# One 128 x 128 scaling per chunk of the RWKV operand [b|k]: GpSimd's TENSOR_SCALAR becomes ScalarE's ACTIVATE

## The chip, the cores and the metric

The kernel runs on one core of a Trainium2 chip. The metric is device time in microseconds (us) of one execution; lower is better. The kernel before took 1404.71 us (median of three runs, 1403.94 to 1408.78).

## The reference: what is computed

One hybrid transformer block over 512 tokens of width 1024, float32. The input is normed and multiplied by `w_in`; three mixers use slices of the result (HGRN2, RWKV-7 and a latent attention, MLA); their outputs are multiplied by branch weights, gated and summed; an output projection and a gated feed-forward layer follow, each with a norm and a residual.

```python
h = rms_norm(x, mix_pre_g[l])
z = h @ w_cols
o_hg = hgrn2_mixer(zq, zf, zi, zog, ...)
o_rw, v_first = rwkv7_mixer(zrw, rwkv_mu[l], ...)
o_mla = mla_mixer(zcq, zckv, zkr, cos, sin, ...)
merged = (g_hg * (o_hg @ w_branch[l, 0]) + g_rw * (o_rw @ w_branch[l, 1])
          + g_mla * (o_mla @ w_branch[l, 2]))
x = x + rms_norm(merged @ w_out[l], mix_post_g[l])
x = x + rms_norm((silu(gate) * up) @ w_ffn_out[l], ffn_post_g[l])
```

The change lies in the RWKV mixer, whose state is updated token by token in the reference:

```python
sa = jnp.einsum('bhvk,bhk->bhv', state, -kk_t)
state = (state * w_t[:, :, None, :] + sa[..., None] * (kk_t * a_t)[:, :, None, :]
         + v_t[..., None] * k_t[:, :, None, :])
```

The kernel does this by chunks of 64 tokens. For each chunk it needs the matrix [b|k] (b is `kk * a`), scaled so that the decay runs to the end of the next chunk. That scaling, one factor for each of 128 channels and each chunk, is what the change moves.

## The kernel before

**Dense products.** All large products run as three TensorE passes: each float32 operand is split into a high part (rounded to fp32r) and a low part, and `mm3` (lines 137, 138 and 139) issues high x high, low x high and high x low into one PSUM tile. A weight slab of 128 x 2 x 256 is loaded by a DMA from SyncE's queue (`wsD`), rounded on ScalarE (`whD`, line 205), and its low part is made on VectorE (`wlD`, line 132). Slabs have three buffers. `stream` walks an output of 256 columns: for each slab two column blocks, for each block two groups of three matmuls. The two PSUM tiles (`mmD`, a pool of two buffers) are copied out on ScalarE when complete (`zst`, line 237, or a tanh at line 251 for the gates) and written to DRAM.

**Tokens.** The dense stream is the filler behind everything else. So that it cannot run ahead, `pace` (line 141) makes each group write a token, a 1 x 1 memset on GpSimd (line 149) that waits for the group's last matmul. The first matmul of a group waits for the token of the group five before it (`PACE = 5`). GpSimd executes in order, so a token stands behind whatever GpSimd is doing.

**RWKV preparation.** Eight pairs of heads (p from 0 to 7) in four groups are prepared while the input projection streams. In `rwkv_prep`, `BK` is a tile of 8 chunks of 128 x 128. It is first the stationary operand of the score products with X (lines 578 to 582, recorded at lines 191 and 194, the lines of a helper that keeps pairs side by side). VectorE masks the scores out of PSUM (lines 584, 585). Then seven of the chunks are scaled in place by the next chunk's decay, `gC[:, c + 1]`, at line 594. They are transposed on TensorE, four at a time and then three, and copied to the group's tile `G` by ScalarE (line 599). `BK` and most temporaries have one buffer. The result goes to DRAM (`rwd`) and is read back in the serial chain over chunks, `rwkv_chain`, which starts after the fourth group.

**Other uses of GpSimd.** It also computes the power -1/2 for every norm (line 279), small memsets (lines 521, 640), and in the chain the decay of the state (line 717).

**Order of the work.** The program is written in lanes: each lane is a range of priorities, and a scheduler with its own estimate of durations sets the order of the instructions on each engine when the kernel is built. Every engine then executes its list in order, waiting where operands are not ready. MLA, in the second half, is interleaved with the dense products of branches 0, 1 and 2 in the same way.

Of the kernel before, what the change touches and what calls it, by code (L numbers as in the profile page):

```python
# [16 lines left out]
AF = mybir.ActivationFunctionType  # L17
ALU = mybir.AluOpType
# [84 lines left out]
class Kern:  # L103
# [391 lines left out]
    def rwkv_prep(self, G, p, q):  # L495
        nc, rt = self.nc, self.rt
        V, A, Pl = nc.vector, nc.scalar, nc.gpsimd
# [34 lines left out]
        gC = self.gC[:, p]  # L532
# [28 lines left out]
        BK = self.t(rt, [P, NC, P], "BK")  # L561
# [29 lines left out]

        n = NC - 1
        for c in range(n):
            Pl.tensor_scalar(BK[:, c], BK[:, c], gC[:, c + 1:c + 2], None, op0=ALU.mult)  # L594
        for cc in range(0, n, 4):
            m = min(4, n - cc)
            pt = self.t(self.pR, [P, 4, P], "pr")
# [768 lines left out]
```

## Time and profile before

| | |
|---|---|
| median of three runs | 1404.71 us |
| lowest, highest | 1403.94, 1408.78 us |
| the profiled execution, its time | 1408.42 us |
| span of its profile | 1406.6 us |
| mean granted TensorE clock | 0.996 |
| TensorE matmul busy | 1354.8 us, 96% of the span |
| VectorE busy | 848.3 us, 60% |
| ScalarE busy | 638.6 us, 45% |
| GpSimd busy | 190.8 us, 14% |
| the changed operation (line 594) | 56 instructions, 47.0 us busy on GpSimd |

Engines are named PE (TensorE matmul), PEld (its weight loads), DVE (VectorE), ACT (ScalarE), POOL (GpSimd) and SP (SyncE). Rows of groups read: line, engine, operation, output <- inputs, shapes, count, then busy us and mean ns of one, then the idle time of the engine just before and what ended it. Matmuls are pipelined and their ends are modelled, so PE at 96% is not PE at its peak; what the profile tells well is when PE had nothing under way. Rows of the waits read: who waited, for whom, total us, times, longest.

### The profile page before, as it was taken

What the parts mean: (1) busy time and instruction counts of PE and PEld (TensorE: products, weight loads), DVE (VectorE), ACT (ScalarE), POOL (GpSimd) and SP (SyncE); (2) the same over time, 40 slices, a digit from 0 to 9 for tenths busy, and PEclk for the clock granted to TensorE, in tenths of its full rate; (3) what the DMA queues carried; (4) which work ended last, traced back from release to release, by engine and by line L of the source; (5) the groups of instructions that cost most, each with busy time, mean ns of one, the idle gap of its engine ahead of it and who ended that gap; (6) DMA issues with size and microseconds to landing.
All of it is one profiled execution on the core that took longest, in us unless ns stands there. A gap on an engine that the chain in (4) does not pass through costs nothing.

```text
span 1406.6 us, 27356 instructions
## 1 busy us (share of the span) xinstructions
PE 1354.8 (96%) x9664; PEld 1103.2 (78%) x9664; DVE 848.3 (60%) x1756; ACT 638.6 (45%) x1259; POOL 190.8 (14%) x1042
## 2 busy tenths in 40 slices
PE   6999999999999999999999999999999999999998
PEld 5777777777777777888788888877888888888886
DVE  5567797797787784575665576655575344343234
ACT  5554546556556453433665354443354333332222
POOL 2122132131222311242210000001010000000000
PEclk9999999999999999999999999999999999999999
DMA  5565467557755777986464555415544333334233
GB/s 180 149 193 144 129 183 227 178 153 218 213 157 155 242 237 227 356 277 208 137 204 147 157 178 168 130 53 173 198 139 135 98 97 92 102 95 156 97 98 105
DMA packets 196025, 231.62 MB, mean 165 GB/s; under 512 B 42672, under 2 KB 137392, under 8 KB 195888
## 3 DMA queue, kind: packets, MB, share of 16 engines
q1 hardware_dynamic: 194496, 226.72, 52.1%
q10 hardware_dynamic: 1392, 3.15, 0.7%
q8 instruction: 76, 1.25, 0.4%
q14 instruction: 61, 0.50, 0.1%
HBM read 169.65 MB, written 60.16 MB: 163 GB/s over the span
## 4 chain that ended last, share of the span: by engine, by line
PE 82%; DMA 6%; DVE 4%; issue 4%; ACT 3%; POOL 1%; SPq 1%; POOLq 0%; DVEq 0%; ACTq 0%
PE mmD L137 18%; PE mmD L138 17%; PE mmD L139 17%; PE po L137 4%; PE po L139 4%; PE po L138 4%; PE pr L194 1%; DMA wsD<-in_w_in_dram 1%; DMA z<-zst 1%; DMA zr<-z 1%; PE pmo L1138 1%; PE pm L137 1%; PE pm L139 1%; PE pm L138 1%; PE ph L843 1%
## 5 line engine op out<-in xcount | busy, mean ns | idle before, releaser
L137 PE MATMUL mmD<-xH,whD 128*128 128x512 f32 (+1 forms) x1232 | 486.2, 397 | 11.9 <-POOL token L149 5.6
L138 PE MATMUL mmD<-xL,whD 128*128 128x512 f32 (+1 forms) x1232 | 474.2, 386 | 0.0
L139 PE MATMUL mmD<-xH,wlD 128*128 128x512 f32 (+1 forms) x1232 | 469.6, 385 | 0.9 <-DVE wlD L132 0.9
L132 DVE TENSOR_TENSOR wlD<-wsD,whD 128x512 fp32r<-128x512 f32 x384 | 263.2, 687 | 292.0 <-ACT whD L205 276.0
L205 ACT CAST whD<-wsD 128x512 fp32r<-128x512 f32 x384 | 236.7, 618 | 375.8 <-PE mmD L138 244.1
L137 PEld LDWEIGHTS mmD<-xH,whD 128*128 128x128 f32 x1232 | 232.0, 189 | 65.2 <-POOL token L149 8.9
L139 PEld LDWEIGHTS mmD<-xH,wlD 128*128 128x128 f32 x1232 | 232.2, 189 | 48.6 <-DVE wlD L132 2.0
L138 PEld LDWEIGHTS mmD<-xL,whD 128*128 128x128 f32 x1232 | 233.5, 190 | 40.1
L149 POOL MEMSET token<- 1x1 f32 x912 | 82.2, 90 | 675.4 <-PE mmD L139 660.1
L139 PE MATMUL po<-whD,fL 128*128 128x512 f32 x176 | 68.6, 390 | 0.0
L138 PE MATMUL po<-wlD,fH 128*128 128x512 f32 x176 | 68.6, 390 | 0.0
L137 PE MATMUL po<-whD,fH 128*128 128x512 f32 x176 | 61.9, 390 | 0.0
L279 POOL TENSOR_TENSOR rrs<-rtm,mhalf 128x1 f32<-128x1 f32 x8 | 4.4, 551 | 402.3 <-DVE rtm L274 368.7
L646 DVE TENSOR_TENSOR invtmp<-inv 64x30 f32<-64x30 f32 (+14 forms) x120 | 38.7, 322 | 17.7 <-DMA inv<-Ld 16.0
L594 POOL TENSOR_SCALAR BK<-BK,gC 128x128 f32<-128x128 f32 x56 | 47.0, 854 | 11.8 <-PE pr L194 11.8
L237 ACT COPY zst<-mmD 128x512 f32<-128x512 f32 x64 | 37.3, 583 | 14.6 <-PE mmD L139 14.4
L647 DVE TENSOR_TENSOR inv<-inv,invtmp 64x30 f32<-64x30 f32 (+14 forms) x120 | 38.4, 320 | 2.2
L139 PEld LDWEIGHTS po<-whD,fL 128*128 128x128 f32 x176 | 33.0, 188 | 7.0
L138 PEld LDWEIGHTS po<-wlD,fH 128*128 128x128 f32 x176 | 33.0, 188 | 7.0
L137 PEld LDWEIGHTS po<-whD,fH 128*128 128x128 f32 x176 | 33.0, 188 | 7.0
L843 PEld LDWEIGHTS ph<-hq,hk 128*32 128x32 f32 x1536 | 17.6, 111 | 18.0 <-issue 9.6
L1136 ACT COPY mpT<-pmt 128x128 f32<-128x128 f32 (+3 forms) x32 | 13.6, 425 | 38.0 <-PE pmt L1134 37.9
(349 smaller groups left out, 1960.1 us busy)
## 6 DMA issues: line engine op xcount, KB each, us to landing
wsD<-in_w_in_dram SPq DMA_DIRECT2D x176, 256.0 KB, 3.4
wsD<-in_w_ffn_in_dram SPq DMA_DIRECT2D x96, 256.0 KB, 2.8
z<-zst SPq DMA_DIRECT2D x63, 256.0 KB, 3.3
rwd<-G SPq DMA_DIRECT2D x28, 512.0 KB, 5.5
G<-rwd SPq DMA_DIRECT2D x28, 512.0 KB, 6.7
wsD<-in_w_branch_dram SPq DMA_DIRECT2D x48, 256.0 KB, 2.9
wsD<-in_w_ffn_out_dram SPq DMA_DIRECT2D x44, 256.0 KB, 2.6
zr<-z SPq DMA_DIRECT2D x26, 256.0 KB, 3.3
```

What stands on the lines that cost most here:

```text
L132: (eng or self.nc.vector).tensor_tensor(dst, src, high.bitcast(F32), op=ALU.subtract)
L137: first = mm(ps, lhsT=lh, rhs=rh, start=start, stop=False)
L138: mm(ps, lhsT=lh, rhs=rl, start=False, stop=False)
L139: return first, mm(ps, lhsT=ll, rhs=rh, start=False, stop=stop)
L149: token = self.nc.gpsimd.memset(self.token, 0.0).ins
L194: last = c()
L205: nc.scalar.copy(h, st)
L237: self.nc.scalar.copy(st[:m], ps)
L594: Pl.tensor_scalar(BK[:, c], BK[:, c], gC[:, c + 1:c + 2], None, op0=ALU.mult)
L646: V.tensor_tensor(tv, cv, rv, op=ALU.mult)
L647: V.tensor_tensor(U[:, :j, j + 1:], U[:, :j, j + 1:], tv, op=ALU.add)
L843: mm(g[b:b + HB, o // P, :], lhsT=k[:, t], rhs=q[:, t], start=True, stop=True)
```

## The change

In the loop over seven chunks of each of the eight pairs, the multiplication by the per-partition scalar is issued on ScalarE as a Copy with a scale instead of on GpSimd:

```diff
         n = NC - 1
         for c in range(n):
-            Pl.tensor_scalar(BK[:, c], BK[:, c], gC[:, c + 1:c + 2], None, op0=ALU.mult)
+            A.activation(BK[:, c], BK[:, c], AF.Copy, scale=gC[:, c + 1:c + 2])
         for cc in range(0, n, 4):
             m = min(4, n - cc)
             pt = self.t(self.pR, [P, 4, P], "pr")
             self.side_by_side(partial(nc.tensor.transpose, pt[:, c], BK[:, cc + c, :], self.ident) for c in range(m))
             A.copy(G["BKT"][:, q, cc:cc + m, :], pt[:, :m])
```

Since the scheduler works from all instructions together, other rows move too. In the program the first pairs keep nearly their order but for the moved operation; from the fourth pair on, matmuls, casts and copies are interleaved differently.

On GpSimd, in the preparation of pair 1 (BK is the operand, token the pacing memset, rs and lw small tiles of the preparation, inv the tile of the inverse), the piece of the difference is:

```order
 L279 TENSOR_TENSOR rs_4895<-ss_4893,mhalf 128x8
-L149 MEMSET token 1x1 x21
-L594 TENSOR_SCALAR BK_4905<-BK_4905,gC_4658 128x128 x4
-L149 MEMSET token 1x1 x4
-L594 TENSOR_SCALAR BK_4905<-BK_4905,gC_4658 128x128 x3
-L149 MEMSET token 1x1 x6
+L149 MEMSET token 1x1 x31
 L640 MEMSET inv_5012 64x32
```

The 31 tokens now follow each other with nothing between them.

On ScalarE, at the same pair (zst is the copy of a finished dense tile out of PSUM, whD the cast of a slab):

```order
 L606 CAST a_4980<-t_858_4977 128x512
 L237 COPY zst_1123<-mmD_1033 128x512
+L594 ACTIVATE BK_4905<-BK_4905,gC_4658 128x128 x4
 L205 CAST whD_1179<-wsD_1177 128x512
 L237 COPY zst_1127<-mmD_1034 128x512
 L830 ACTIVATE hsg_7588<-hz_7586 128x512
+L594 ACTIVATE BK_4905<-BK_4905,gC_4658 128x128 x3
 L205 CAST whD_1201<-wsD_1199 128x512
 L599 COPY G_4683<-pr_4961 128x4x128
```

The first batch of four now stands between the two copies that free the two dense PSUM tiles of one stream, and ahead of a slab's cast.

On TensorE, in the sixth of the eight MLA heads (pm is its score tile, mmD with xH a group of branch 1, mmD with oH a group of branch 2, which needs finished heads), before:

```order
L1122 MATMUL pm_11412<-krL_10418,qr_10455 128x256
L138 MATMUL mmD_10180<-xL_1602_9833,whD_10228 128x512
L139 MATMUL mmD_10180<-xH_1594_9825,wlD_10229 128x512
L137 MATMUL mmD_10181<-xH_1593_9824,whD_10228 128x512
L138 MATMUL mmD_10181<-xL_1601_9832,whD_10228 128x512
L139 MATMUL mmD_10181<-xH_1593_9824,wlD_10229 128x512
```

and in the changed program:

```order
L1122 MATMUL pm_11412<-krL_10418,qr_10455 128x256
L1138 MATMUL pmo_11259<-mpT_11346,mv_10588 128x128 x4
L1118 MATMUL pm_11434<-uh_1975_11387,uh_1969_11370 128x384
L1119 MATMUL pm_11434<-ul_1976_11388,uh_1969_11370 128x384
L1120 MATMUL pm_11434<-uh_1975_11387,ul_1970_11371 128x384
L1121 MATMUL pm_11434<-krH_10417,qr_10455 128x384
L1122 MATMUL pm_11434<-krL_10418,qr_10455 128x384
L137 MATMUL mmD_11762<-oH_1768_10682,whD_11810 128x512
```

The groups of branch 1 are used up earlier in the changed program, so the sixth head has almost no dense work between its own products.

## The prediction

> **What bounds the kernel now.** I read first the page's busy times and the measured stretches, to find which engine sets the end, and where.
>
> ```profile
> span 1406.6 us, 27356 instructions
> 40.00:500.00 460.00, 441.44 (x3740) 344.93 (x3739) 353.28 (x787) 253.81 (x508) 108.79 (x537) 1.00 0.59 178
> L594 POOL TENSOR_SCALAR BK<-BK,gC 128x128 f32<-128x128 f32 x56 | 47.0, 854 | 11.8 <-PE pr L194 11.8
> L594 POOL TENSOR_SCALAR BK<-BK,gC x56: 593/604/2934, 75.8 to 483.5; 128x128 f32<-128x128 f32 x56
> ```
>
> The columns of the second row are the stretch, its length, then busy us of PE, PEld, DVE, ACT and POOL, clock, DMA share and GB/s. PE works 441.44 of 460 us while the RWKV preparation runs, so the whole stage holds 460 - 441.44 = 18.56 us in which PE had nothing under way. Line 594 takes 47.0 us of GpSimd in 56 instructions, all between 75.8 and 483.5 us. The question is not what those 47 us cost GpSimd, which is idle most of the time, but how much of PE's idle time they cause. Second I read who PE waited for in this stage:
>
> ```profile
> PE mmD L137 <- POOL token L149: 4.3, 5, 1.8
> PE pr L557 <- ACT t L555: 2.6, 2, 1.6
> PE pr L191 <- DVE G L585: 2.0, 3, 0.9
> ```
>
> Waits for a token are the largest kind, 4.3 us in five places. Third I looked at GpSimd at those five places, to see what the late tokens stood behind:
>
> ```profile
> 110.87 1.67 POOL L279 TENSOR_TENSOR rs<-ss,mhalf 128x8 f32<-128x8 f32 x1 [2.11 <-DVE ss L550]
> 185.69 1.38 POOL L279 TENSOR_TENSOR hrs<-htm,mhalf 128x4 f32<-128x4 f32 x1 [3.34 <-DVE htm L274]
> 274.33 0.12 POOL L521 MEMSET lw<- 128x8 f32 x1 [6.77 <-ACT lh L491]
> 281.99 1.80 POOL L279 TENSOR_TENSOR rs<-ss,mhalf 128x8 f32<-128x8 f32 x1 [4.88 <-DVE ss L550]
> 300.63 4.39 POOL L594 TENSOR_SCALAR BK<-BK,gC 128x128 f32<-128x128 f32 x4 [1.62 <-PE pr L194]
> 305.11 0.50 PE L137 MATMUL mmD<-xH,whD 128*128 128x512 f32 x1 [0.44 <-POOL token L149]
> ```
>
> Four of the five are other things: the powers of line 279 and the memset of line 521, each waiting up to 6.77 us for its own operand with tokens behind it. These stay on GpSimd. Only at 300.63 is it line 594, and the stall there is 0.44 us. Why so little is seen at a batch without a stall:
>
> ```profile
> 75.82 2.85 POOL L594 TENSOR_SCALAR BK<-BK,gC 128x128 f32<-128x128 f32 x4 [0.31 <-PE pr L194]
> 78.62 0.38 POOL L149 MEMSET token<- 1x1 f32 x3
> 82.61 0.09 POOL L149 MEMSET token<- 1x1 f32 x1 [0.61 <-PE mmD L139]
> 83.31 0.09 POOL L149 MEMSET token<- 1x1 f32 x1 [0.61 <-PE mmD L139]
> 188.65 3.50 POOL L594 TENSOR_SCALAR BK<-BK,gC 128x128 f32<-128x128 f32 x4 [0.31 <-PE pr L194]
> 419.70 4.67 POOL L594 TENSOR_SCALAR BK<-BK,gC 128x128 f32<-128x128 f32 x4 [0.31 <-PE pr L194]
> ```
>
> Two tokens in a free-running stream are 0.70 us apart (82.61 to 83.31), the length of one group. A group waits for the token of the fifth before it, so GpSimd may be blocked for about five groups, 3.5 us, before PE notices, and longer where small matmuls stand in between. A batch of four takes 2.85 us, or 4 x 0.604 = 2.4 undisturbed. Only three rows reach 3.5 us (3.50, 4.39 and 4.67), and in the waits only 4.39 shows as a stall.
>
> **Tokens freed: the largest gain there can be.** I measured the eight stretches that hold all the batches; the sum of their rows is
>
> ```profile
> 75.00:90.00 15.00, 14.58 (x83) 11.36 (x82) 9.75 (x15) 6.07 (x9) 5.74 (x21) 1.00 0.57 171
> 474.00:486.00 12.00, 11.55 (x163) 9.06 (x162) 11.55 (x23) 3.56 (x6) 7.51 (x18) 1.00 0.68 212
> sum 107.00, PE 103.89 PEld 80.46 DVE 93.39 ACT 49.28 POOL 57.19; mean PE 12.99 PEld 10.06 DVE 11.67 ACT 6.16 POOL 7.15
> sum 107.00, POOL 47.04; mean POOL 5.88
> ```
>
> (first and last of eight, and the sums; the last row counts line 594 alone, so all 47.04 us are inside). PE idles 107.00 - 103.89 = 3.11 us in all of them, whatever the cause. The gain from GpSimd's side is therefore between 0 and 3.11 us; I take the one seen stall, -0.4 us.
>
> **What ScalarE pays.** No row shows a 128 x 128 ACTIVATE from SBUF with a scale operand. The nearest:
>
> ```profile
> L901 ACT ACTIVATE hkT<-ph,hrs x32: 356/368/379, 187.9 to 663.7; 128x128 f32<-128x128 f32 x32
> L491 ACT CAST lh<-lst 128x128 fp32r<-128x128 f32 x16 | 4.8, 298 | 4.6 <-PE pr L138 3.6 <-DVE hq L867 0.5 <-DMA lst<-in_rwkv_a_up_dram 0.3
> L421 ACT ACTIVATE v<-zr,omm 128x512 f32<-128x512 f32 x8 | 5.8, 725 | 10.8 <-DMA zr<-z 7.7 <-DMA grw<-v 1.9 <-issue 1.1
> L205 ACT CAST whD<-wsD 128x512 fp32r<-128x512 f32 x384 | 236.7, 618 | 375.8 <-PE mmD L138 244.1
> ```
>
> Line 901 is the same operation and size, but reads PSUM: 0.368 us. Line 491 reads SBUF without a scale: 0.298; the scale adds 0.725 - 0.618 = 0.107 (line 421 against 205), which makes 0.405. Between 0.298 and 0.405 I take 0.37, line 901. A batch of four is then 1.5 us, of three 1.1, and 56 x 0.37 = 20.7 us go to an engine that is busy 49.28 of the 107 us there; with them 70.0, or 65%. ScalarE as a whole has room. [...]
>
> What the batches stand in front of matters more. Behind them in ScalarE's order are slab casts and the PSUM copies zst. The casts are covered: line 205's idle time ended mostly with PE freeing a buffer (244.1 us), so a cast is done well before PE wants it, and 1.5 us fit. The copies have less room, since only two PSUM tiles serve the stream:
>
> ```profile
> L237 ACT COPY zst<-mmD x64: 562/582/612, 31.4 to 528.5; 128x512 f32<-128x512 f32 x63, 64x512 f32<-64x512 f32 x1
> PE mmD L137 <- ACT zst L237: 2.9, 2, 2.2
> ```
>
> A stream's second tile ends two groups (1.4 us) after its first, and the next stream wants that buffer two groups later still. The second copy takes 0.58, so it may start 1.4 - 0.58 = 0.82 us late. Where a batch and a cast stand between the two copies, the second starts 0.58 + 1.1 + 0.62 = 2.30 us after the first for three operations, 2.70 for four: 0.9 or 1.3 late, 0.1 or 0.5 too much. The changed order has five such places (pairs 0, 1, 2, 5, 7; in the fourth of these another two copies stand between too, 0.25 us each, 0.6 too much): 3 x 0.1 + 0.5 + 0.6 = 1.4 us. Small products of the preparation often fill the interval on PE, and the two waits of the whole run (2.9 us) show that late copies mostly cost nothing. Bounds 0 and 1.4; I take +0.5.
>
> **The scaled operand itself** is ready earlier: 1.5 instead of 2.4 to 4.7 us per batch. It feeds transposes, copies and a DMA to DRAM whose reader is the chain after 550 us. Hidden by the dense stream; no gain. If that cover were gone it would be 1 to 3 us per pair.
>
> **The moved order.** In the sixth MLA head branch 1's filler is gone, as in the seventh before. What an unfilled head costs is read from the last two:
>
> ```profile
> 902.50:924.50 22.00, 22.00 (x118) 18.74 (x117) 13.67 (x33) 9.02 (x21) 1.50 (x17) 1.00 0.41 124
> 924.50:936.40 11.90, 11.71 (x75) 10.30 (x73) 7.71 (x24) 6.62 (x16) 0.27 (x3) 1.00 0.14 45
> 936.40:952.00 15.60, 12.21 (x73) 9.53 (x71) 8.18 (x25) 6.61 (x16) 0.35 (x4) 1.00 0.00 1
> ```
>
> The sixth (902.5) idles 0; the seventh, unfilled but with the eighth to overlap, 11.90 - 11.71 = 0.19; the eighth, alone, 3.39. The sixth has a successor, so +0.2, bounds 0 and 3.4.
>
> **Sum.** -0.4 + 0.5 + 0.2 = +0.3 us on the profiled execution's 1408.42 us. That execution lies 1408.42 - 1404.71 = 3.71 above the median, so the median becomes 1405.0: no change. A measurement of this kernel tells about 0.5% from no change, 7 us.
>
> **Rivals.** (1) *The copies become the bound*, slower. On GpSimd a batch waited 11.8 us / 16 = 0.74 us for the score products. If on ScalarE it waits as long at the head of the queue, with a copy of a PSUM tile behind it, each place adds 0.74: 5 x 0.74 + 1.4 = 5.1 us; if both batches of all eight pairs hit a copy at 0.6 us, 16 x 0.6 = 9.6 and 1414. It decides once the second copy starts over 0.82 us late. For it: the five places. Against it: late copies cost 2.9 us in the whole run, though table loads and activations already stand before them. (2) *The new order avoids waits*, faster. The stage's 18.56 us of idle are mostly operands that came a little later than the scheduler thought; another interleaving draws them anew. Half of them gone gives 1404.7 - 9.3 = 1395.4. For it: thousands of rows moved. Against it: nothing aims at those waits, and it can as well go the other way, 1414. (3) *VectorE was held up too.* Line 594's longest is 2934 ns against 593 at the least, so GpSimd waited inside the instruction while VectorE ran; if VectorE lost time likewise, products that wait for it come sooner, and all 3.11 us of the eight stretches go: 1401.6, still within no change. Against it, VectorE's masks keep their length during the batch at 300.63:
>
> ```profile
> 78.91 0.68 DVE L584 TENSOR_TENSOR G<-pr,cst 64x512 f32<-64x512 f32 x1
> 302.72 0.68 DVE L584 TENSOR_TENSOR G<-pr,cst 64x512 f32<-64x512 f32 x1
> ```
>
> [...]
>
> **How the numbers follow.** No change, 0.68, of which 0.1 is rival 3 near 1402; rival 1 or an unlucky order, 0.17, near 1414; rival 2, 0.15, near 1395. So faster 0.15, same 0.68, slower 0.17. The bounds of the terms alone reach from 1405.0 - 2.7 - 0.5 - 0.2 = 1401.6 to 1405.0 + 0.4 + 0.9 + 3.2 = 1409.5; runs of before spread over 4.8 us, and the order adds its own. A range of 1396 to 1413.5 takes in the no-change band (1397.7 to 1411.7) and part of each tail.
>
> **What would show it.** GpSimd's busy time falls by about 47 us to some 144, ScalarE's rises by about 21 to 659; line 594 appears at 0.30 to 0.41 us. Token waits remain, behind lines 279 and 521. PE's idle time in the stage from 40 to 500 us stays near 18.6 us. It would be wrong if PE's waits for tokens vanish altogether, if PE's waits for zst grow beyond 3 us, or if the idle time of the stage moves by more than 7 us either way.

## The result, and the profile after

The changed kernel takes 1414.59 us (median of 6 runs, 1413.14 to 1422.61), the kernel before 1408.26 us beside it (6 runs, 1403.94 to 1410.28). The ratio on record is 1.0063 with a 95% interval of 1.0046 to 1.0079: **slower by 0.6%**. (The ratios here are those on record; they are not quotients of the medians, which would be 1.0045 here.) The forecast had called up to 0.5% no change, and the interval reaches just into that band. 1414.59 us lies 1.1 us above the upper end of the range. Part of the distance to the forecast of 1405.0 is no effect of the change: the forecast started from a median of 1404.71 us, and the six runs of the kernel before have 1408.26.

The rows of after that answer to those shown of before: the page's head and busy times, the measured stretch from 40 to 500 us, the group of line 594, and who TensorE waited for.

```profile
span 1412.4 us, 27345 instructions
PE 1356.7 (96%) x9664; PEld 1104.4 (78%) x9664; DVE 846.0 (60%) x1756; ACT 655.6 (46%) x1315; POOL 143.8 (10%) x986
40.00:500.00 460.00, 434.28 (x3679) 339.94 (x3678) 344.53 (x768) 262.98 (x546) 60.33 (x469) 0.99 0.59 176
L594 ACT ACTIVATE BK<-BK,gC 128x128 f32<-128x128 f32 x56 | 18.3, 392 | 4.1 <-PE pr L194 3.9
PE pr L547 <- ACT t L543: 8.8, 4, 3.4
PE pr L191 <- DVE G L585: 3.8, 3, 2.3
PE mmD L137 <- ACT zst L237: 3.0, 4, 1.2
PE mmD L137 <- POOL token L149: 1.0, 2, 0.6
```

The operation did what the diff says: 47.0 us left GpSimd (190.8 to 143.8), 18.3 us came to ScalarE. Waits for a token fell from 5.6 us in the whole run to 1.0. Yet in the same 460 us PE got through 3679 matmul records where it had 3740, and was idle 460 - 434.28 = 25.7 us where it had been 18.6. A wait that was small before is now the largest of the stage: the products of line 547 (the sum of squares of k, at the head of each pair) wait 8.8 us for the Square of line 543 on ScalarE, 1.2 us before. The two rows of before:

```profile
PE pr L547 <- ACT t L543: 1.2, 2, 0.9
PE mmD L137 <- POOL token L149: 5.6, 6, 1.8
```

The four longest of these waits, from the timeline (start, length, engine, line, then in brackets the idle time before and what ended it), are three at line 547 and one at line 191:

```profile
274.99 1.05 PE L547 MATMUL pr<-cst,t 128*128 128x2 f32 x8 [2.61 <-ACT t L543]
340.00 1.23 PE L547 MATMUL pr<-cst,t 128*128 128x2 f32 x5 [3.35 <-ACT t L543]
428.20 0.46 PE L191 MATMUL pr<-G,BK 64*128 64x128 f32 x2 [2.34 <-DVE G L585]
460.53 1.07 PE L547 MATMUL pr<-cst,t 128*128 128x2 f32 x8 [2.57 <-ACT t L543]
```

No scaling of line 594 stands near the three of line 547. These are the heads of pairs 4, 5 and 7. In pair 4, ScalarE's queue stands at line 421 until a DMA has brought `zr` (4.84 us at 271 us), and the Square comes after it:

```profile
271.10 0.73 ACT L421 ACTIVATE k<-zr,omm 128x512 f32<-128x512 f32 x1 [4.84 <-DMA zr<-z]
274.21 0.73 ACT L543 ACTIVATE t<-k,vT 128x512 f32<-128x512 f32 x1
```

That wait for `zr` is not what is new: in the kernel before it is longer at the same place (5.78 us, until 273.35 us), and there TensorE reaches line 547 at 277.12 us without a wait. So two explanations are open. **Theory O**: the order of all the other instructions, which the scheduler drew anew, makes the loss. **Theory Q**: the operation on ScalarE delays what stands behind it in ScalarE's queue.

There is also something that no row of waits shows. Behind the wait at 274.99 us the matmuls run at half speed for a while:

```profile
276.22 0.40 PE L138 MATMUL mmD<-xL,whD 128*128 128x512 f32 x1
276.46 0.39 PE L139 MATMUL mmD<-xH,wlD 128*128 128x512 f32 x1
...
277.17 0.63 PE L139 MATMUL mmD<-xH,wlD 128*128 128x512 f32 x1
277.60 0.63 PE L137 MATMUL mmD<-xH,whD 128*128 128x512 f32 x1
278.02 0.63 PE L138 MATMUL mmD<-xL,whD 128*128 128x512 f32 x1
...
280.56 0.39 PE L138 MATMUL mmD<-xL,whD 128*128 128x512 f32 x1
280.80 0.40 PE L139 MATMUL mmD<-xH,wlD 128*128 128x512 f32 x1
```

They start 0.43 us apart (277.17 to 277.60) instead of 0.24. In this time PE counts as busy (3.00 of the 3.00 us from 277.2 to 280.2 us, at a granted clock of 0.50), so a sum of idle time misses it.

### The profile page after: what moved, and what is told of

It reads as the page before. It is cut to its first block, busy times and chain, and to the rows that moved or that the text cites. A ratio compares the mean times of both kernels' runs of the same rounds, so it can differ in the third digit from the quotient of the medians.

```text
span 1412.4 us, 27345 instructions
## 1 busy us (share of the span) xinstructions
PE 1356.7 (96%) x9664; PEld 1104.4 (78%) x9664; DVE 846.0 (60%) x1756; ACT 655.6 (46%) x1315; POOL 143.8 (10%) x986
## 4 chain that ended last, share of the span: by engine, by line
PE 77%; DMA 9%; DVE 6%; ACT 4%; issue 3%; SPq 1%; POOL 0%; DVEq 0%; POOLq 0%; ACTq 0%
PE mmD L137 17%; PE mmD L139 16%; PE mmD L138 16%; PE po L138 4%; PE po L139 4%; PE po L137 4%; DMA wsD<-in_w_in_dram 2%; DMA z<-zst 2%; DMA zr<-z 2%; PE pr L194 1%; PE pm L137 1%; PE pm L138 1%; DVE wlD L132 1%; PE pm L139 1%; PE pmo L1138 1%
## 5 line engine op out<-in xcount | busy, mean ns | idle before, releaser
L1129 ACT ACTIVATE mp<-pm,mmx,scq 128x128 f32<-128x128 f32 (+3 forms) x32 | 19.8, 620 | 18.9 <-DVE mmx L1126 18.7
```

Source lines behind the costliest of these rows:

```text
L1129: A.activation(p[:, :n], s_, AF.Exp, bias=mx, scale=self.scq[:, i:i + 1], accum_out=sm)
```

## The experiments

Each ratio is to the kernel before on the same chip, with its 95% interval. Kernels called pinned carry a list of all the traced instructions, and one dependency per instruction holds each engine to the sequence of that list, whatever the scheduler would do; the order is then free of the operation's engine. The code is shortened here. "Old order" is that of the kernel before, "new order" that of the changed one, and the decay stands in the place that the other kernel has for it.

```diff
     Kern(ctx, tc, ins, args[-1], dbg).run()
+    pin(tc)
+def pin(tc):
+    ...                                  # the list and the instructions by number
+    last = {}
+    for n in order:                      # numbers of the instructions
+        i = traced[f"I-{n}"]; e = str(i.engine)
+        if e in last:
+            tc.add_manual_dep(i, last[e], NoSync, reason="order")
+        last[e] = i.name
```

### 1 to 4: engine and order, each with both values

> The kernel before with every engine's instruction order written down as it was and enforced. A control: both theories expect the time of before, ratio 1.000 within 0.002, since neither an instruction nor its place differs.

> The scaling on ScalarE, everything else in the order of the kernel before (the scaling stands in ScalarE's queue at the place it had among all engines' instructions). Theory O, the new order of the other instructions is what costs: no loss, ratio 0.995 to 1.002, waits of the sum-of-squares products (line 547) near the 1.2 us of before. Theory Q, the scalings in ScalarE's queue hold back what stands behind them: ratio 1.004 to 1.008 like the changed kernel.

> The scaling on GpSimd as before, but every other instruction in the changed kernel's order. Theory O: slow like the changed kernel, ratio 1.004 to 1.009, line 547 waits 8 us or more. Theory Q: ratio 0.998 to 1.002, since nothing was put into ScalarE's queue.

> The changed kernel with its own order written down and enforced. A control: ratio 1.004 to 1.008 by both theories.

| ratio to the kernel before | old order | new order |
|---|---|---|
| decay on GpSimd | 1.0012 (0.9998 to 1.0026) | 1.0062 (1.0048 to 1.0076) |
| decay on ScalarE | 0.9986 (0.9975 to 0.9998) | 1.0055 (1.0039 to 1.0071) |

Medians: 1406.68, 1413.29, 1403.95 and 1412.57 us, against 1405.64 us of the kernel before. The corners stand for the two kernels themselves, and pinning alone moved neither beyond its interval. Across the table the order costs 0.5 to 0.7%. Down the table ScalarE costs nothing: in the old order it is 2.7 us shorter, in the new order the difference (0.07%) is inside the intervals.

The record also has the mean granted clock of each run. The medians in the old order are 0.9945 (GpSimd) and 0.9965 (ScalarE), in the new order 0.9890 and 0.9895. Over 1406 us the difference is 1406 x 0.0055 = 7.7 us and 1406 x 0.0070 = 9.8 us of clock, and the medians of the times differ by 6.6 and 8.6 us. So the half clock alone is about as large as the whole loss. TensorE's waits grew too, and the 7.7 and 9.8 us of clock are already more than the 6.6 and 8.6 us by which the times differ; how the loss divides between waits and clock is not shown.

The waits follow the order too: here GpSimd has the decay and the new order is pinned, and then ScalarE and the old order.

```profile
PE pr L547 <- ACT t L543: 8.8, 5, 3.7
```

```profile
PE pr L547 <- ACT t L543: 0.8, 2, 0.7
PE mmD L137 <- POOL token L149: 5.6, 5, 1.7
```

The line 547 waits 8.8 us with not one decay in ScalarE's queue, and 0.8 us with all 56 in it. Theory Q falls; theory O stands.

### 5 and 6: moving the work that waits

In the new order, the products of line 547 of pairs 4, 5 and 7 are put five dense groups later (pair 4 shown); the second kernel also puts dense groups between tiny products at 672 us (shown with experiment 11).

```diff
-L547 MATMUL pr_5684<-cst,t_983_5681 128x2 x4
 L137 MATMUL mmD_1916<-xH_12_113,whD_1963 128x512
...
 L139 MATMUL mmD_1916<-xH_14_115,wlD_1986 128x512
+L547 MATMUL pr_5684<-cst,t_983_5681 128x2 x4
```

> The changed kernel's instructions in the changed kernel's order, except that in pairs 4, 5 and 7 the four products of L547 and the few TensorE instructions that depend on them stand five dense groups later, so that the Square of L543 is done when TensorE reaches them. Theory W (most of the 0.5 to 0.6% that the order costs is these three waits of 2.6 to 3.4 us and the half-clock windows that follow them): the waits of L547 for L543, 8.8 us in the changed kernel, fall under 2 us, the half-clock windows at 277 and 339 us go, and the ratio to the kernel before falls from 1.0055 to between 0.998 and 1.002. Rival M (the work that L547 waits for is late for everybody, and the wait moves to the next instruction that needs it): the wait appears at L557 or L191 with about the same length and the ratio stays between 1.004 and 1.007.

> The same as the kernel with the products of L547 moved behind five dense groups, and four dense groups are also moved up into the stretch of tiny products (L731 and L1001) at about 672 to 681 us, behind which the changed kernel ran 6.8 us at half the clock. If the half clock there is caused by TensorE doing only tiny products, the window at 680 us goes and the time falls by a further 2 to 3.5 us (about 0.2% of the time); if that window has another cause, it stays and the time is that of the kernel without the four groups moved.

The first: 1420.08 us against 1408.52, 1.0083 (1.0066 to 1.0101). The second: 1414.12 us, 1.0044 (1.0029 to 1.0059). The wait of line 547 went (0.8 us left), and in pair 5 the next step of the same chain took its place, longer than before (the second line; the first is a product of the HGRN2 mixer):

```profile
343.51 0.50 PE L843 MATMUL ph<-hq,hk 128*32 128x32 f32 x32 [2.25 <-DVE hk L868]
351.09 1.11 PE L557 MATMUL pr<-cst,t 128*128 128x128 f32 x4 [4.42 <-ACT t L555]
```

Theory W falls and rival M holds in kind, with a price beyond its range (1.0083 where 1.004 to 1.007 was expected). The likely reason is that delaying one product delays the whole chain of squares, power and scaling behind it. The second kernel is 0.39% or 6.0 us shorter than the first, where 2 to 3.5 us were expected; experiment 11 tries its other edit alone and finds 0.22%. The intervals are wide enough for both, so the rest may be noise and is not explained.

### 7 and 8: the same change without a pinned list

Undone by pairs of heads and left to the scheduler, one pair decides. With the decay on ScalarE in pair 3 alone, TensorE's order differs from the kernel before's in 2671 lines of the difference, from the changed kernel's in 36. With it everywhere but in pair 3, it differs from the kernel before's in 36.

```diff
-            Pl.tensor_scalar(BK[:, c], BK[:, c], gC[:, c + 1:c + 2], None, op0=ALU.mult)
+            if p == 3: A.activation(BK[:, c], ...)     # experiment 8: p != 3
+            else:      Pl.tensor_scalar(BK[:, c], ...)
```

> Seven of the 56 decays, those of pair 3 alone, are on ScalarE; the scheduler then writes nearly the changed kernel's order for the other instructions (36 lines of TensorE's order differ from the changed kernel's, 2671 from the kernel before's). Theory O (the order costs, not the engine): the whole loss is there with an eighth of the moved work, a ratio between 1.004 and 1.007, with the waits of L547 for L543 at 7 to 10 us. Theory Q (each decay on ScalarE holds up ScalarE's queue): an eighth of the loss, a ratio of 1.000 to 1.002.

> The other 49 decays are on ScalarE, those of pair 3 stay on GpSimd; the scheduler then writes nearly the order of the kernel before (36 lines of TensorE's order differ). Theory O: no loss, and seven eighths of the 0.1 to 0.25% that the op itself won under the pinned old order: a ratio between 0.997 and 1.000, faster than both kernels. Theory Q: seven eighths of the loss, a ratio of 1.004 to 1.006.

Pair 3 alone: 1415.03 us against 1408.52, 1.0055 (1.0034 to 1.0077). All but pair 3: 1404.43 us, 0.9976 (0.9961 to 0.9990). Seven moved operations, with the order that they bring, have the whole loss; the other 49 come with a gain. In the waits, pair 3 alone and then all but pair 3:

```profile
PE pr L547 <- ACT t L543: 12.2, 4, 4.6
```

```profile
PE mmD L137 <- POOL token L149: 5.1, 5, 1.6
PE pr L547 <- ACT t L543: 0.5, 2, 0.4
```

This rules out that the pinning made the result of experiments 1 to 4.

### 9, 10 and 11: where in the order

At about 511 us both orders have issued the same set of instructions. Two kernels change from one order to the other at that point; a third is the new order with four dense groups moved up into a stretch of tiny products.

```diff
+ORDER = new[:5243] + old[5243:]        # experiment 9
+ORDER = old[:5243] + new[5243:]        # experiment 10
 # experiment 11, in TensorE's new order:
+L137, L138, L139 MATMUL mmD_4060 ... x6
 L1001 MATMUL pm_10331<-ones_64,msq_10354 128x1 x4
 L1001 MATMUL pm_10331<-ones_64,msq_10363 128x1 x2
 L731 MATMUL zus_7412<-zsb_7393,G_7161 64x64 x16
+L137, L138, L139 MATMUL mmD_4155 ... x6
 L1001 MATMUL pm_10331<-ones_64,msq_10363 128x1 x2
 L1001 MATMUL pm_10331<-ones_64,msq_10370 128x1 x4
-(the twelve dense matmuls stood here)
```

> All 56 decays on ScalarE; every engine follows the changed kernel's order up to one point and the kernel before's order from there on. The point is where both orders have issued the same set of instructions (behind two of the 128x128 products of L891, at 510.7 us in the kernel before and 518.4 us in the changed kernel). Theory F (the loss is made in the RWKV stage before that point): a ratio of 1.003 to 1.006. Theory T (it is made behind that point, above all in the stretch of tiny products at 672 to 681 us and the half clock behind it): a ratio of 0.997 to 1.000.

> The other half: the kernel before's order up to that point and the changed kernel's order behind it, all 56 decays on ScalarE. Theory F: 0.997 to 1.000, as with the whole old order. Theory T: 1.003 to 1.006. If both halves cost, both kernels lie between, at 1.001 to 1.003.

> The changed kernel in its own order, with only the four dense groups moved up into the tiny products of L731 and L1001 at about 672 to 681 us; the products of L547 stand where the changed kernel has them. If these groups were worth the 6 us by which the kernel with both edits was shorter than the one with the L547 edit alone: 1407 us, a ratio of 1.000 to 1.002, and no half-clock window at 680 us. If they are worth only the half clock that they take away: 3.4 us, 1.002 to 1.004. If the 6 us came from elsewhere: 1.0045 to 1.006.

Against 1405.57 us of the kernel before: 1410.87 us, 1.0036 (1.0024 to 1.0048); 1408.59 us, 1.0022 (1.0010 to 1.0034); 1410.48 us, 1.0033 (1.0021 to 1.0045). Over the old order with the same operation (0.9986), the first half of the new order costs 0.50% and the second, by experiment 10, 0.36%. The second number is not clean. At the point of change experiment 10 has a wait that neither whole order has there, with matmuls of 0.63 us behind it (the granted clock is 0.91 from 500 to 520 us):

```profile
514.07 0.79 PE L893 MATMUL ph<-hst,hq 128*128 128x128 f32 x2 [3.32 <-DVE hst L886]
```

Seen from the other side, the whole new order against experiment 9, the second half costs 1.0055 - 1.0036 = 0.19%, no more than the intervals. In the profiles of the two kernels themselves the point lies at 510.67 us before and 518.42 us after, 7.7 us later. From there to the first output product (lines below, at experiment 17) it takes 983.67 - 510.67 = 473.0 us before and 989.27 - 518.42 = 470.9 us after. So the first half carries the loss; that the second adds to it is not shown.

One place in the second half does cost time. Experiment 11 took 0.22% (about 3 us; the intervals are 0.12 and 0.16% each way) off the new order by moving four groups, as its middle case said. The measured stretches of 20 us at that place, in the pinned new order and with the groups moved:

```profile
680.00:700.00 20.00, 20.00 (x113) 16.55 (x114) 11.57 (x26) 7.92 (x13) 2.99 (x17) 0.81 0.30 87
```

```profile
680.00:700.00 20.00, 18.98 (x129) 16.00 (x130) 12.17 (x27) 10.91 (x19) 5.90 (x20) 1.00 0.42 126
```

The granted clock (third number from the end) goes from 0.81 to 1.00: 20 x 0.19 = 3.8 us of clock, against 1.0 us more of idle time. In the new order PE was not waiting in this stretch. It had run small products since 672.7 us, those of lines 1001 and 731 among them (128 x 1 and 64 x 64), with waits of 0.70, 0.38 and 0.27 us in the changed kernel, and then met its dense matmuls at half speed, 0.43 us apart (from the timeline of the changed kernel):

```profile
679.57 1.60 PE L1001 MATMUL pm<-ones,msq 128*128 128x1 f32 x8 [0.27 <-ACT msq L999]
681.03 0.77 PE L137 MATMUL mmD<-xH,whD 128*128 128x512 f32 x1
681.60 0.63 PE L138 MATMUL mmD<-xL,whD 128*128 128x512 f32 x1
682.03 0.63 PE L139 MATMUL mmD<-xH,wlD 128*128 128x512 f32 x1
```

### 13, 14 and 15: the first half in three stretches

Each kernel has the new order in one stretch and the old one elsewhere, decay on ScalarE.

```diff
+ORDER = new[:3477] + old[3477:]                      # 13: up to the head of pair 5
+ORDER = old[:3477] + new[3477:4483] + old[4483:]     # 14: pairs 5 and 6
+ORDER = old[:4483] + new[4483:5243] + old[5243:]     # 15: pair 7
```

> All decays on ScalarE; the changed kernel's order up to the head of pair 5 (the first 3477 of the list, about 340 us, with the waits of L547 at 272 and 337 us), the kernel before's order behind it. The first 511 us of the changed order cost 0.36% over the kernel before, and 0.50% over the same operation in the old order (0.9986). Theory S (the loss sits at the heads of pairs 4 and 5, where two of the three long waits of L547 are): a ratio of 1.002 to 1.005. Theory E (it is spread evenly over the three stretches): each of the three kernels at 0.9995 to 1.001.

> The changed kernel's order only in the second stretch (list places 3477 to 4483: the rest of pair 5 and pair 6), in which the changed kernel has no wait of L547 over 1 us. Theory S: as the old order, 0.997 to 1.000. Theory E: 0.9995 to 1.001.

> The changed kernel's order only in the third stretch (list places 4483 to 5243: pair 7, with the wait of 2.6 us of L547 at 458 us and up to about 511 us). Theory S: one wait of 2.6 us and perhaps a half-clock window of 3.4 us (1.7 us lost), 0.1 to 0.3% over the old order: 0.9995 to 1.0015. Theory E: 0.9995 to 1.001; no loss at all here (0.998) speaks for the first stretch alone.

Against 1406.26 us: 1411.30 us, 1.0037 (1.0023 to 1.0052); 1407.51 us, 1.0011 (0.9997 to 1.0025); 1401.46 us, 0.9968 (0.9955 to 0.9981). The first stretch carries the loss of the half.

The second came out 0.25% over the old order, beyond what theory S allowed. Its profile has at 424 us the wait of line 191 for line 585 that the changed kernel has at 428 us (1.87 us; experiment 2 has none there), then matmuls of 0.63 us and a granted clock of 0.91 from 420 to 440 us, 1.8 us. Together that is about the 0.25%, in one profile.

The third came out 0.18% under the old order, below the ranges of both theories, though its interval and that of the old order overlap. In its profile the stretch itself is not shorter: line 891 at the end of it stands at 508.22 us, in experiment 2 at 507.57. What is missing is a wait right behind it, 2.31 us for a copy zst in experiment 2. Such waits at the point of change show that these parts do not simply add. The wait of line 547 in pair 7 is not there in experiment 15, and only 0.44 us in experiment 4, which has the changed kernel's own order, where the changed kernel's profile had 2.57; so it does not go with the order alone.

In the first stretch the loss can be followed. From the head of pair 4 to that of pair 5 the old order (ScalarE, pinned) takes 337.05 - 274.69 = 62.4 us, the new one 342.65 - 275.45 = 67.2. The timelines and one stretch, old order first:

```profile
272.07 0.50 PE L137 MATMUL mmD<-xH,whD 128*128 128x512 f32 x1 [1.45 <-POOL token L149]
274.69 1.05 PE L547 MATMUL pr<-cst,t 128*128 128x2 f32 x8
275.60 0.48 PE L138 MATMUL mmD<-xL,whD 128*128 128x512 f32 x1
337.05 1.05 PE L547 MATMUL pr<-cst,t 128*128 128x2 f32 x8
275.00:342.00 67.00, 65.27 (x607) 51.42 (x606) 55.07 (x127) 43.36 (x90) 9.51 (x63) 0.97 0.53 155
```

```profile
275.45 1.78 PE L547 MATMUL pr<-cst,t 128*128 128x2 f32 x8 [3.17 <-ACT t L543]
277.66 0.63 PE L138 MATMUL mmD<-xL,whD 128*128 128x512 f32 x1
281.50 0.63 PE L138 MATMUL mmD<-xL,whD 128*128 128x512 f32 x1
342.65 1.66 PE L547 MATMUL pr<-cst,t 128*128 128x2 f32 x7 [4.51 <-ACT t L543]
275.00:342.00 67.00, 62.68 (x554) 49.51 (x554) 49.39 (x114) 38.41 (x83) 7.80 (x62) 0.94 0.51 146
```

In both the Square starts at about the same time (273.90 and 274.67 us), and ScalarE's wait for `zr` before it is longer in the old order (6.33 us) than in the new (5.41). The old order still has dense groups to run there, after a token wait of 1.45 us; the new one has run them already, stands for 3.17 us, and then runs at half the clock (matmuls 0.63 us long until 282 us). In the 67 us the idle time grows by 65.27 - 62.68 = 2.6 us and the clock gives 67 x (0.97 - 0.94) = 2.0 us less, as far as two decimals tell: 4.6 of the 4.8 us. The whole experiment is 0.51% or about 7 us over the old order, so some 2 us of it are not located.

### 12, 16 and 18: what the tokens cost

In pinned orders the waits for tokens can be dropped without a move of anything else.

```diff
-PACE = 5
+PACE = 10 ** 6
```

> All decays on ScalarE in the pinned order of the kernel before, and no dense group waits for a token any more (PACE is a number that is never reached; the token memsets stay in GpSimd's queue, and all data dependences stay). This takes away the whole of what tokens in GpSimd's queue can cost TensorE: 5.6 us of waits for a token in the kernel before. If these waits are time lost: 3 to 5.6 us less than the same order with the waits, a ratio of 0.994 to 0.997. If what the token holds back would wait for its weights or its bank anyway: 0.998 to 1.000, and waits for whD, wlD or zst of 3 us and more in the place of the tokens'.

> The decays on GpSimd, the kernel before's order pinned, no dense group waits for a token. If the 0.1 to 0.25% that the decay gained on ScalarE in the old order came through tokens that stood behind the decays, it is gone here: the same time as with the decay on ScalarE and no token wait, a ratio of 0.994 to 0.997. If it came another way (the copies of the decayed operand start earlier, since ScalarE needs 0.39 us for an operation and GpSimd longer), the difference stays: 0.997 to 0.9985.

> The changed kernel in its own order, without the waits for tokens. In that order they are 1.0 us of TensorE's waiting, in the old order 5.6. If the old order's token waits have become waits of L547 for L543: nothing is gained, a ratio of 1.004 to 1.006 with the waits of L547 at 8 us and more. If the tokens are still what places the waits (a group held back by a token fills the later wait): a gain of 2 us and more, under 1.003.

| | with token waits | without |
|---|---|---|
| old order, GpSimd | 1.0012 | 0.9964 (0.9948 to 0.9980), 1400.85 us |
| old order, ScalarE | 0.9986 | 0.9956 (0.9943 to 0.9970), 1399.63 us |
| new order, ScalarE | 1.0055 | 1.0062 (1.0043 to 1.0080), 1414.51 us |

In the old order the tokens cost 0.3 to 0.5%, and without them the engine of the decay makes a difference of 0.08%, which these intervals don't tell from none. That points to the tokens as the way by which the move helped in the old order. It is not shown: the gain fell from 0.26 to 0.08%, no more than the intervals, and the token waits were 6.7 us on GpSimd and 5.6 us on ScalarE, which is 1.1 us of the 2.7 us between those kernels. In the new order dropping the waits does nothing, as expected if the waits have become those for the Square of line 543 (8.1 us here).

### 17: the gains put together

Decay on ScalarE, new order in the stretch of pair 7 alone, no token waits.

> All decays on ScalarE, the kernel before's order except for the stretch of pair 7, which has the changed kernel's, and no dense group waits for a token. If the two gains are of different waits they add: 0.9968 and another 0.3 to 0.4%, a ratio of 0.992 to 0.995. If the stretch of pair 7 only helped by avoiding a token wait that is gone here anyway: 0.995 to 0.997, as without it (0.9956).

1397.52 us against 1406.23, 0.9945 (0.9925 to 0.9964). That lies in the range for two gains that add, but the interval also holds 0.9956, the time without token waits alone, so it is not shown that they add. This version beats both kernels. The first output product (line 137, tile `po`) begins at 972.5 us in its profile; before and after the change it stood at

```profile
983.67 1.09 PE L137 MATMUL po<-whD,mH 128*128 128x512 f32 x4
```

```profile
989.27 1.09 PE L137 MATMUL po<-whD,mH 128*128 128x512 f32 x4
```

## Why the prediction was wrong

**What bounds the kernel** was read rightly: PE sets the end, and the 47 us of line 594 are not what counts.

**Tokens freed** was right in its bounds and low in its value. Taken: -0.4 us from the one stall seen at line 594, bound 3.11. Measured in the old order, with everything that the move of the operation does: 1403.95 - 1406.68 = -2.7 us, within the bound. The stall that it named is there: pinned with the decay on GpSimd, the group behind the same batch waits

```profile
303.23 0.50 PE L137 MATMUL mmD<-xH,whD 128*128 128x512 f32 x1 [0.91 <-POOL token L149]
```

and with the decay on ScalarE it does not. Where the other 1.8 us come from is not shown. One reading of the lines was wrong: six batches reach 3.5 us in the kernel before, not three (also 3.52, 3.71 and 3.73 us, at 242, 195 and 475 us), but only the one at 300.63 us has a stall behind it, as the prediction said.

**What ScalarE pays** was small, as said, and the terms' sizes were close: 0.388 us for one operation where 0.37 was taken, and 18.3 us of ScalarE where 20.7 was forecast.

```profile
L594 ACT ACTIVATE BK<-BK,gC x56: 385/388/414, 75.8 to 487.3; 128x128 f32<-128x128 f32 x56
```

Successive ones overlap: 56 x 0.392 = 21.95 us of single lengths make 18.3 us busy, 3.65 us over 40 successions, 91 ns each.

The **copies zst** took +0.5 of 0 to 1.4 us. Their waits are 3.0 us after and 2.9 before, and 4.1 and 3.8 us with the old order pinned (ScalarE and GpSimd). So they cost some 0.3 us at most, and rival 1, the copies as the bound, is not what happened.

**The moved order** is the step that failed. The prediction priced it at one place, the sixth MLA head (+0.2 us, at most 3.4), and put the rest of the reordering at nothing in the sum. "Thousands of rows moved" stood only as a rival that could go either way: 0.15 for faster, and 0.17 for slower, shared with rival 1. The MLA part was indeed harmless: from 700 to 980 us PE is busy 276.28 of 280 us before and 275.43 after. But the order of the RWKV stage and of its chain costs 0.5 to 0.7%, some 7 to 10 us, by experiments 1 to 4, and 7 and 8. Above all it is the first half, up to the heads of pairs 4 and 5 (experiments 9 and 13), where TensorE has used up its dense groups, waits for line 543 and then runs at half the clock (matmuls 0.63 us long instead of 0.39). The whole loss is this term; the operation itself made the kernel faster in the old order and changed nothing that can be told in the new.

**Rivals.** Rival 2 said that another interleaving draws the waits anew and that it can go to 1414 as well as to 1395; it went to 1414.6. The mechanism is right, its sign was open in the profile of before, and that the figure agrees so closely is luck: it stood for 9.3 us on a base of 1404.71, the runs have 6.3 us on one of 1408.26, and the lost clock was not in it. Rival 3 (VectorE) is not settled: in the pinned old order DVE's busy time is 848.1 us with the decay on GpSimd and 847.3 on ScalarE, and TensorE's waits for line 585 fall from 2.0 to 1.0 us, so it can be part of the 2.7 us but not large.

**What would show it.** GpSimd at 143.8 (144 said) and ScalarE at 655.6 (659 said) came out. Token waits did not remain: 1.0 us in the whole run, and the two behind lines 279 and 521 at 274 and 282 us went with the order, not with the operation, since with ScalarE and the old order 5.6 us are still there. PE's idle time in the stage moved by 25.7 - 18.6 = 7.1 us, just past the 7 us that the prediction had named as the sign of its being wrong.

What could have been known before: the comparison of the two programs showed that thousands of rows had moved from the fourth pair on, and the prediction itself said that such an order could go to 1414. What only the experiments show is how wide the spread is that an order alone makes: with the decay on ScalarE and the token waits kept, the orders tried here measured 0.9968 to 1.0083.

## What to carry to other kernels

Where a scheduler orders the program, moving one operation to another engine is two changes: the operation, and a new order of everything else. Price them apart, and measure them apart: pin the order, or find (as with pair 3) the few instructions that flip it. A gain of 0.3% in the operation can be lost twice over in an order that was drawn by chance, and a wait that a change removes can become the next operand's wait, as it did in experiment 5. An order put together from two has waits of its own at the point of change, so parts measured in this way need not add up.

## What the runs showed of the hardware

The half clock was not expected. In the profiles shown here the granted clock falls to one half for a few us: after the change it is 0.50 from 277.12 to 280.53 us, and in experiment 13 the matmuls are 0.43 us apart from 277.66 to 281.93 us, with a granted clock of 0.92 from 255 to 300 us. Both come with a few us in which PE did no dense work, 3.9 us after the change (272.0 to 275.9), 5.2 us in experiment 13 (271.9 to 277.1). It counts as busy time (3.41 of the 3.41 us after the change), so a sum of PE's waits shows only part of what the stalls cost here: in the stretch of pairs 4 and 5, 2.6 us of waiting and 2.0 us of clock. It also came with little waiting, from 679.89 us on, in the last of 8.3 us of small products (672.7 to 681.0); with dense groups put between them the clock of 680 to 700 us is 1.00 (experiment 11) where the same order without them has 0.81. In these stretches the matmuls are 0.43 us apart instead of 0.24. In the row of 680 to 700 us after the change

```profile
680.00:700.00 20.00, 20.00 (x115) 16.34 (x116) 10.89 (x25) 8.14 (x15) 3.36 (x20) 0.83 0.31 89
```

the clock is 0.83, so 20 x 0.17 = 3.4 us are lost. The clock is 0.50 from 679.89 to 686.72 us, and half of those 6.83 us is the same 3.4. The waits ahead of these two were short: at 274.99 us one of 2.61 us, with small products on both sides of it, and in the 6 us from 674 to 680 us PE was idle for 6.00 - 4.57 = 1.43 us in all, in gaps of at most 0.70 us. What sets the clock to one half, and for how long, is not shown.
